# Building h in one kernel of a Griffin-style block: fourteen whole projection blocks, eight of them split, and first parts of fifteen mLSTM blocks

## The chip, the cores and the metric

The kernel runs on one core of a Trainium2 chip. The metric is the device time of one execution in microseconds (us); several runs are compared by their median. All data is fp32.

## The reference, cut to what matters

```python
mod = c_act @ ada_w + ada_b
shift_m, scale_m, gate_m, shift_f, scale_f, gate_f = jnp.split(mod[:, None, :], 6, axis=-1)
h = rms_norm(x, norm_mix_w) * (1 + scale_m) + shift_m
proj = h @ w_in
(a_q, a_k, a_v, a_o, a_i, a_f, b_qkv, b_z, b_beta, b_a, merge) = jnp.split(proj, IN_SPLITS, axis=-1)
...
h_a = bidirectional(mlstm_chunkwise, (q_a, k_a, v_a), (log_i[0], log_f[0]), (log_i[1], log_f[1]))
...
o_b = bidirectional(gated_delta_chunkwise, (q_b, k_b, v_b), (beta[0], log_decay[0]), (beta[1], log_decay[1]))
...
x = x + gate_m * ((g_a * y_a + g_b * y_b) @ w_out)
hf = rms_norm(x, norm_ffn_w) * (1 + scale_f) + shift_f
gt, up = jnp.split(hf @ w_gate_up, 2, axis=-1)
x = x + gate_f * ((jax.nn.silu(gt) * up) @ w_down)
```

There are 256 tokens, 2048 channels, 4 mLSTM heads (keys and queries of 256 channels) and 16 heads of the delta rule (GDN). The change lies in how the columns of `proj` are computed: one block row of 128 columns for the gates, 48 for the delta rule's k, q, v, and 16 for the mLSTM's keys and queries (two of each for a head).

## The kernel before, in words

**Building h.** h has 16 blocks `b` of 128 channels by 256 tokens. To modulate a block, DVE needs a scale and a shift for each of its channels: each is the sum of a row of 2048 weights times silu(c). These rows (`ra`, two tiles of 1 MB for each b, five buffers) stream from DRAM through SP's queue (function `loads`), DVE multiplies and sums them (`summed`, L548; `scale` is the first of the two calls). ACT then writes the block, `x[:, b]` (L587), and its value rounded to fp32r, `hh` (L588); DVE writes the remainder `hl` (L593), one step later than `hh`, and multiplies the next block by the norm's factor (`spread`, L553).

**The first projections.** While h is built, TensorE needs work: 16 block rows of `w_in` (N0; the gates, twelve for the first four GDN heads, three for the mLSTM's head 0) come with each b as a tile `raw` of 128 x 16 x 128 (1 MB, three buffers). For each, one fp32 matmul accumulates `raw[:, o]` times `x[:, b]` in one of 16 halves of the eight PSUM banks, `first[o]` (L595). In the last step only four block rows are done so; the twelve others are "split": ACT rounds the weights to `wh` (L603), DVE subtracts to get `wl` (L604), and three fp32r passes, wh·hh, wh·hl and wl·hh, take the place of one fp32 matmul (L606 to L608).

**Order.** `order()` keeps an instruction in the program's order among those of its engine that are also marked. Nearly all ACT and DVE instructions of this loop are marked. What isn't marked, the scheduler may place earlier. Each engine works through its queue in that order.

**After it.** `gates` computes decay and gates from `first[0]`, evicts `first[1..12]` to the convolution's pads (`evict`, L411), and copies the three mLSTM blocks to `ev0` and to DRAM, `kq_d[0]`. The remaining projections are jobs in a list, `fills`, of which the program takes a step (`fill(n)`) wherever the delta rule leaves TensorE free: `tjob` for wide ones (512 columns) and `fjob` for one block row. `fjob` (L172) loads 16 blocks (1 MB), splits eight at a time (ACT L181, DVE L183) and runs 48 passes (L186 to L188), with one `yield` for each eight blocks; `done` evicts the result. `a_qk(h, j)` is such a job for the mLSTM's keys and queries; before, 13 of them run (`rest`), with `keep_f` evicting to `evf` (two buffers) and ACT's queue storing to `kq_d`. `pump` in each step adds up further rows of the modulation. `mlstm(h)` loads `kq_d[h]` later through POOL's queue (L988), which also carries the delta rule's small transfers (`inst_d` L722 and others).

Of the kernel before, what the change touches and what calls it, by code (L numbers as in the profile page):

```python
# [9 lines left out]
F32 = mybir.dt.float32  # L10
# [5 lines left out]
P = 128  # L16
# [10 lines left out]
N0 = 4 + 3 * GRP  # L27
# [25 lines left out]
def hybrid_block(ctx: ExitStack, tc: tile.TileContext, xr, nfr, crow, pk_d, cst_d, ada2, ada4, win0, winb, wint, wba, wbb, wo, wgu, wd, out, dbg=None):  # L53
# [18 lines left out]
    def order(ins, yes=True):  # L72

        return tc.keep_in_program_order(ins) if yes else ins
# [97 lines left out]
    def fjob(name, src, done):  # L172

        ps = acc_ps.tile([P, 512], F32, tag="acc", name=f"acc_{name}")
        o = ps[:, :T]
        raw = raw_tile([P, KB, P], f"raw_{name}")
        nc.sync.dma_start(raw, src)
        for k0 in range(0, KB, 8):
            wh = st.tile([P, 8, P], F32R, tag="wh", bufs=3, name=f"wh_{name}_{k0}")
            wl = st.tile([P, 8, P], F32R, tag="wl", bufs=3, name=f"wl_{name}_{k0}")  # L180
            S.activation(wh, raw[:, k0 : k0 + 8], AF.Copy)  # L181
            settle()
            order(V.tensor_tensor(wl, raw[:, k0 : k0 + 8], wh.bitcast(F32), ALU.subtract), beside[0])  # L183
            for k in range(8):
                kk = k0 + k
                PE.matmul(o, wh[:, k], woven(hh[:, kk]), start=kk == 0, stop=False)  # L186
                PE.matmul(o, wh[:, k], woven(hl[:, kk]), start=False, stop=False)  # L187
                PE.matmul(o, wl[:, k], woven(hh[:, kk]), start=False, stop=kk == KB - 1)  # L188
            pump()
            if k0:  # L190
                done(o.rearrange("p (c h) -> p h c", h=2))
            yield True
# [179 lines left out]
    def keep_f(dst, name):  # L372
        def done(ps):
            ev = evp.tile([P, T], F32, tag="evf", bufs=2, name=f"ev_{name}")
            S.activation(ev.rearrange("p (h c) -> p h c", h=2), ps, AF.Copy)
            S.dma_start(dst, ev)
        return done
# [11 lines left out]
    def a_qk(h, j):  # L389
        return fjob(f"a{h}_{j}", winb[36 + 4 * h + j], keep_f(kq_d[h][j], f"a{h}_{j}"))  # L390
# [14 lines left out]
    for i in range(4):  # L405
        rest += [m_job(1, i), a_vo(1, i)] + [a_qk(i, j) for j in range(4) if i or j == 3] + [m_job(0, i)]

    def evict(o):

        if o <= 3 * GRP:  # L410
            S.activation(pads[(o - 1) % NP_][:, 2 : T + 2], first[o], AF.Copy)  # L411

    def gates(w0, zz, first):
# [75 lines left out]
        ev0 = w0.tile([P, D + 2], F32, tag="ra", bufs=5, name="ev0")  # L489
        for j in range(3):  # L490
            S.activation(ev0[:, j * T : (j + 1) * T], first[13 + j], AF.Copy)
        S.dma_start(kq_d[0][0:3].rearrange("j p t -> p j t"), ev0[:, : 3 * T].rearrange("p (j t) -> p j t", j=3))
# [14 lines left out]
    with ExitStack() as s0:  # L507
        w0 = pool(s0, "w0")

# [19 lines left out]
        def loads(b):  # L529
            ra = [w0.tile([P, D + 2], F32, tag="ra", bufs=5, name=f"ra{b}_{i}") for i in range(2)]  # L530
            raw = st.tile([P, N0, P], F32, tag="raw", bufs=3, name=f"raw0_{b}")
# [3 lines left out]
            n = 4 if b == KB - 1 else N0  # L535
            for o in range(0, N0, n):
                order(nc.sync.dma_start(raw[:, o : o + n], win0[b, :, o : o + n]))
            return ra, raw
# [16 lines left out]
        ra, raw = loads(0)  # L555
# [17 lines left out]
        banks += [gps(f"first{i}") for i in range(4, 8)]  # L573
# [4 lines left out]

        for b in range(KB):
            if b:  # L580
                ra, raw = loads(b)
                m2 = scale(b, ra)
# [6 lines left out]
            if b < KB - 1:  # L589
                spread(b + 1)  # L590
            for bb in ((b - 1,) if b < KB - 1 else (b - 1, b)):
                if bb >= 0:
                    order(V.tensor_tensor(hl[:, bb], x[:, bb], hh[:, bb].bitcast(F32), ALU.subtract))  # L593
            for o in range(N0 if b < KB - 1 else 4):
                PE.matmul(  # L595
                    first[o], raw[:, o], x[:, b], start=b == 0 and o % 2 == 0, stop=b == KB - 1 and o % 2 == 1
                )

        wh = [st.tile([P, 8, P], F32R, tag="wh", bufs=3, name=f"wh_first{i}") for i in range(2)]
        wl = [st.tile([P, 8, P], F32R, tag="wl", bufs=3, name=f"wl_first{i}") for i in range(2)]  # L600
        for o0 in range(4, N0, 4):
            w = [a[o0 // 8][:, o0 % 8 : o0 % 8 + 4] for a in (wh, wl)]
            order(S.activation(w[0], raw[:, o0 : o0 + 4], AF.Copy))  # L603
            order(V.tensor_tensor(w[1], raw[:, o0 : o0 + 4], w[0].bitcast(F32), ALU.subtract))  # L604
            for o in range(o0, o0 + 4):
                PE.matmul(first[o], w[0][:, o - o0], hh[:, KB - 1], start=False, stop=False)  # L606
                PE.matmul(first[o], w[0][:, o - o0], hl[:, KB - 1], start=False, stop=False)
                PE.matmul(first[o], w[1][:, o - o0], hh[:, KB - 1], start=False, stop=o % 2 == 1)  # L608


        nc.sync.dma_start(pk, pk_d)
        zz = w0.tile([P, T], F32, name="zz")
        opened = gates(w0, zz, first)
# [998 lines left out]
def _arrays(x, c, ada_w, ada_b, norm_mix_w, w_in, mlstm_b_i, mlstm_b_f, mlstm_norm_w, gdn_conv_w,  # L1612
# [32 lines left out]
    for h in range(NH_A):  # L1645
# [24 lines left out]
        "win0": np.ascontiguousarray(win[[*range(13), 49, 50, 51]].transpose(2, 1, 0, 3)),  # L1670
# [25 lines left out]
```

## Time and profile before

| | |
|---|---|
| median of 3 runs | 1948.41 us (1947.84 to 1948.59) |
| profiled execution | 1949.3 us, its span 1947.4 us |
| PE busy | 1920.7 us (99%) |
| DVE, ACT, POOL busy | 1406.5 (72%), 1032.7 (53%), 124.1 us (6%) |
| moved by DMA | 485.68 MB, mean 249 GB/s |
| the loop over b | first matmul at 19.28 us, last one of the stage at 135.63 us |

The span runs from the first to the last instruction; the run's time lies 1.9 us above it. PE is TensorE's matmuls, PEld its weight loads, DVE VectorE, ACT ScalarE, POOL GpSimd, SP the engine whose queue issues most loads. A busy share is an average over stages: the building of h is limited by other things than the rest. In a line in order of time stand the start and the length in us, the engine, the line of the code (L595), the operation, the written and read tiles, and in brackets how long the engine had been idle and what released it.

### The profile page before, as it was taken

To read this page: it belongs to the slowest core of one execution; us is meant where nothing else is said; L and a number is where in the kernel's file an instruction comes from. 1 tells how busy PE (TensorE), PEld (TensorE's weight loads), DVE (VectorE), ACT (ScalarE), POOL (GpSimd) and SP (SyncE) were. 2 spreads that over 40 slices of the span, in tenths; PEclk is the share of its full clock that TensorE was granted. 3 is DMA by queue.
4 is the path that set the end of the run, shared out by engine and by line. 5 is a ranking of instruction groups with operands and counts; after the bars stand their busy time and mean duration, and the time that the engine had idled before them with its cause. 6 is when DMAs were issued, how large, how long until landed. Compare 5 with 4: busy or idle time off the path is not lost.

```text
span 1947.4 us, 27209 instructions
## 1 busy us (share of the span) xinstructions
PE 1920.7 (99%) x10436; PEld 1704.7 (88%) x10436; DVE 1406.5 (72%) x2084; ACT 1032.7 (53%) x1564; POOL 124.1 (6%) x223
## 2 busy tenths in 40 slices
PE   8999999999999999999999999999999999999997
PEld 7888889998999899889788888888888888888886
DVE  6788886898788789877577988765665655555554
ACT  3147656765776587565544444644444444444443
POOL 0001220111011101120100000200000000000000
PEclk9999999999999999999999999999999999999999
DMA  9997676666666767686777998577677665565553
GB/s 398 421 358 236 188 257 247 207 230 226 233 213 206 244 216 237 208 296 243 254 290 267 357 348 322 201 248 253 242 251 258 240 218 198 205 206 210 196 208 136
DMA packets 80773, 485.68 MB, mean 249 GB/s; under 512 B 11433, under 2 KB 17137, under 8 KB 26625
## 3 DMA queue, kind: packets, MB, share of 16 engines
q1 hardware_dynamic: 64368, 451.02, 64.2%
q0 software_dynamic: 8672, 17.88, 4.4%
q10 hardware_dynamic: 7602, 15.03, 2.0%
q8 instruction: 82, 1.34, 0.3%
q14 instruction: 49, 0.40, 0.1%
HBM read 467.07 MB, written 16.82 MB: 248 GB/s over the span
## 4 chain that ended last, share of the span: by engine, by line
PE 88%; DVE 4%; DMA 4%; ACT 2%; issue 1%; POOL 0%; SPq 0%; DVEq 0%; POOLq 0%
PE acc_up L249 4%; PE acc_up L248 4%; PE acc_up L247 4%; PE acc_gt L248 4%; PE acc_d L248 4%; PE acc_gt L249 4%; PE acc_d L247 4%; PE acc_d L249 4%; PE acc_gt L247 4%; DMA ra<-ada 3%; PE acc_b L186 3%; PE acc_b L188 3%; PE acc_b L187 3%; PE acc_o L247 2%; PE acc_o L249 2%; PE acc_o L248 2%
## 5 line engine op out<-in xcount | busy, mean ns | idle before, releaser
L215 DVE TENSOR_TENSOR wl_d<-raw_d,wh_d 128x1024 fp32r<-128x1024 f32 x88 | 107.7, 1225 | 105.9 <-ACT wh_d L213 105.9
L215 DVE TENSOR_TENSOR wl_up<-raw_up,wh_up 128x1024 fp32r<-128x1024 f32 x88 | 107.7, 1225 | 100.7 <-ACT wh_up L213 100.7
L215 DVE TENSOR_TENSOR wl_gt<-raw_gt,wh_gt 128x1024 fp32r<-128x1024 f32 x88 | 107.7, 1224 | 76.9 <-ACT wh_gt L213 76.9
L186 PE MATMUL acc_b<-hh,wh_b 128*128 128x256 f32 x576 | 162.7, 283 | 0.0
L213 ACT ACTIVATE wh_d<-raw_d 128x1024 fp32r<-128x1024 f32 x88 | 92.9, 1056 | 126.8 <-PE acc_d L248 118.0
L188 PE MATMUL acc_b<-hh,wl_b 128*128 128x256 f32 x576 | 159.4, 277 | 0.1
L187 PE MATMUL acc_b<-hl,wh_b 128*128 128x256 f32 x576 | 159.1, 276 | 0.0
L213 ACT ACTIVATE wh_gt<-raw_gt 128x1024 fp32r<-128x1024 f32 x88 | 92.9, 1056 | 121.7 <-PE acc_gt L248 75.7
L213 ACT ACTIVATE wh_up<-raw_up 128x1024 fp32r<-128x1024 f32 x88 | 92.8, 1056 | 108.0 <-PE acc_up L248 77.0
L125 DVE SCALAR_TENSOR_TENSOR ada<-ada,crow 128x2048 f32<-128x2048 f32 x64 | 146.2, 2284 | 0.0
L247 PE MATMUL acc_up<-wh_up,hfh 128*128 128x512 f32 x352 | 133.4, 379 | 0.0
L248 PE MATMUL acc_up<-wh_up,hfl 128*128 128x512 f32 x352 | 133.4, 379 | 0.0
L249 PE MATMUL acc_up<-wl_up,hfh 128*128 128x512 f32 x352 | 133.4, 379 | 0.0
L247 PE MATMUL acc_gt<-wh_gt,hfh 128*128 128x512 f32 x344 | 131.6, 383 | 0.0
L248 PE MATMUL acc_gt<-wh_gt,hfl 128*128 128x512 f32 x344 | 130.5, 379 | 0.3 <-DVE hfl L1473 0.3
L248 PE MATMUL acc_d<-wh_d,ffl 128*128 128x512 f32 x344 | 130.5, 379 | 0.0
L249 PE MATMUL acc_gt<-wl_gt,hfh 128*128 128x512 f32 x344 | 130.4, 379 | 0.0
L247 PE MATMUL acc_d<-wh_d,ffh 128*128 128x512 f32 x344 | 130.4, 379 | 0.0
L249 PE MATMUL acc_d<-wl_d,ffh 128*128 128x512 f32 x344 | 130.4, 379 | 0.0
L595 PE MATMUL first<-x,raw 128*128 128x256 f32 x488 | 109.5, 385 | 5.4 <-ACT x L587 5.4
L595 PEld LDWEIGHTS first<-x,raw 128*128 128x128 f32 x488 | 93.0, 192 | 22.0 <-ACT x L587 9.4
L187 PEld LDWEIGHTS acc_b<-hl,wh_b 128*128 128x128 f32 x576 | 111.4, 193 | 0.1
(403 smaller groups left out, 5296.1 us busy)
## 6 DMA issues: line engine op xcount, KB each, us to landing
ada<-ada SPq DMA_DIRECT2D x64, 1024.0 KB, 5.0
raw_gt<-wgu SPq DMA_DIRECT2D x44, 1024.0 KB, 4.9
raw_up<-wgu SPq DMA_DIRECT2D x44, 1024.0 KB, 4.9
raw_d<-wd SPq DMA_DIRECT2D x44, 1024.0 KB, 4.8
raw_b<-winb SPq DMA_DIRECT2D x36, 1024.0 KB, 5.2
ra<-ada SPq DMA_DIRECT2D x30, 1025.0 KB, 14.9
raw_z<-wint SPq DMA_DIRECT2D x16, 1024.0 KB, 4.9
raw_v<-wint SPq DMA_DIRECT2D x16, 1024.0 KB, 5.4
```

Of the source, the lines that this page charges most:

```text
L125: order(V.scalar_tensor_tensor(raw, raw, 1.0, row_c[:, :D], ALU.mult, ALU.mult, accum_out=mod[:, c : c + 1]))
L186: PE.matmul(o, wh[:, k], woven(hh[:, kk]), start=kk == 0, stop=False)
L187: PE.matmul(o, wh[:, k], woven(hl[:, kk]), start=False, stop=False)
L188: PE.matmul(o, wl[:, k], woven(hh[:, kk]), start=False, stop=kk == KB - 1)
L213: order(S.activation(wh, raws[u][:, k0 : k0 + 2], AF.Copy), early)
L215: order(V.tensor_tensor(wl, raws[u][:, k0 : k0 + 2], wh.bitcast(F32), ALU.subtract), early or beside[0])
L247: order(PE.matmul(ps[t], xh[:, kk, c], woven(wh[:, k]), start=kk == 0, stop=False), early and steps > 1)
L248: PE.matmul(ps[t], xl[:, kk, c], woven(wh[:, k]), start=False, stop=False)
L249: PE.matmul(ps[t], xh[:, kk, c], woven(wl[:, k]), start=False, stop=kk == last)
L595: PE.matmul(first[o], raw[:, o], x[:, b], start=b == 0 and o % 2 == 0, stop=b == KB - 1 and o % 2 == 1)
```

## The change

The loop now carries 14 block rows: the gates, the twelve of the first four GDN heads, and one mLSTM key block. Six of them (NPL) stay fp32 matmuls; the other eight are split in every step, so ACT makes `wh` and DVE `wl` for 128 x 1024 weights in each. Since the passes of step b read `hl[:, b]`, `hl` is now made in the same step. Results of split blocks lie with even and odd tokens apart in PSUM, and the evictions reorder them.

The 14 rows take seven banks. In the eighth (`apart`), steps b = 3 to 13 compute first parts of the 15 other mLSTM blocks: two blocks each for b = 3 to 6, of their first four channel blocks, and one each for b = 7 to 13, of its first eight. Their weights (`ex`, 512 KB a step) are loaded after `raw` into two buffers that later stages own (`sz`, `ev`), and split too. `put` evicts a step's parts on ACT in the next step to `some`, which is stored to `kq_d` by four transfers after the loop; the gates' small tiles (pool `w1`) take over its memory. The 15 jobs `a_qk` (13 before) then begin at channel block 4 or 8 (`k0` in `fjob`), and their result is added to the one in DRAM by a transfer of POOL's queue (`accum_op`). The eleven steps with partial blocks add 88 blocks of 128 x 128 to the loop, while the jobs have 152 where they had 208.

```diff
FB = FF // P
...
 GRP = 4
-N0 = 4 + 3 * GRP
+N0 = 14
+NPL = 6
...
 PK_ADAB = 0
...
         if more:
...
-    def fjob(name, src, done):
+    def fjob(name, src, done, k0=0):
...
         raw = raw_tile([P, KB, P], f"raw_{name}")
-        nc.sync.dma_start(raw, src)
-        for k0 in range(0, KB, 8):
-            wh = st.tile([P, 8, P], F32R, tag="wh", bufs=3, name=f"wh_{name}_{k0}")
-            wl = st.tile([P, 8, P], F32R, tag="wl", bufs=3, name=f"wl_{name}_{k0}")
-            S.activation(wh, raw[:, k0 : k0 + 8], AF.Copy)
+        nc.sync.dma_start(raw[:, k0:], src[:, k0:])
+        first_ = k0
+        while k0 < KB:
+            k1 = min(k0 + 8 - k0 % 8, KB)
+            wh = st.tile([P, 8, P], F32R, tag="wh", bufs=3, name=f"wh_{name}_{k0}")[:, : k1 - k0]
+            wl = st.tile([P, 8, P], F32R, tag="wl", bufs=3, name=f"wl_{name}_{k0}")[:, : k1 - k0]
+            S.activation(wh, raw[:, k0:k1], AF.Copy)
             settle()
-            order(V.tensor_tensor(wl, raw[:, k0 : k0 + 8], wh.bitcast(F32), ALU.subtract), beside[0])
-            for k in range(8):
-                kk = k0 + k
-                PE.matmul(o, wh[:, k], woven(hh[:, kk]), start=kk == 0, stop=False)
+            order(V.tensor_tensor(wl, raw[:, k0:k1], wh.bitcast(F32), ALU.subtract), beside[0])
+            for kk in range(k0, k1):
+                k = kk - k0
+                PE.matmul(o, wh[:, k], woven(hh[:, kk]), start=kk == first_, stop=False)
                 PE.matmul(o, wh[:, k], woven(hl[:, kk]), start=False, stop=False)
...
             pump()
-            if k0:
+            k0 = k1
+            if k0 == KB:
                 done(o.rearrange("p (c h) -> p h c", h=2))
...
             S.dma_start(dst, ev)
...
-    def keep_f(dst, name):
+    def keep_f(dst, name, more=True):
         def done(ps):
...
             S.activation(ev.rearrange("p (h c) -> p h c", h=2), ps, AF.Copy)
-            S.dma_start(dst, ev)
+            if more:
+                G.dma_start(dst, ev, accum_op=ALU.add)
+            else:
+                S.dma_start(dst, ev)
         return done
...
     def z_job(g, early=0):
...
         return fjob(f"b{h}_{j}", winb[3 * (h - GRP) + j], lambda ps: gdn_conv(h, j, ps))
...
     def a_qk(h, j):
-        return fjob(f"a{h}_{j}", winb[36 + 4 * h + j], keep_f(kq_d[h][j], f"a{h}_{j}"))
+        e = 4 * h + j - 1
+        return fjob(f"a{h}_{j}", winb[37 + e], keep_f(kq_d[h][j], f"a{h}_{j}"), 4 if e < 8 else 8)
...
         return tjob(
...
     for i in range(4):
-        rest += [m_job(1, i), a_vo(1, i)] + [a_qk(i, j) for j in range(4) if i or j == 3] + [m_job(0, i)]
+        rest += [m_job(1, i), a_vo(1, i)] + [a_qk(i, j) for j in range(4) if i or j] + [m_job(0, i)]
...
         if o <= 3 * GRP:
-            S.activation(pads[(o - 1) % NP_][:, 2 : T + 2], first[o], AF.Copy)
+            pd = pads[(o - 1) % NP_][:, 2 : T + 2]
+            if o < NPL:
+                S.activation(pd, first[o], AF.Copy)
+            else:
+                S.activation(pd.rearrange("p (h c) -> p h c", h=2), first[o].rearrange("p (c h) -> p h c", h=2), AF.Copy)
...
         evict(1)
...
         V.tensor_copy(tr[96:104], ex[R, :, 1])
-        ev0 = w0.tile([P, D + 2], F32, tag="ra", bufs=5, name="ev0")
-        for j in range(3):
-            S.activation(ev0[:, j * T : (j + 1) * T], first[13 + j], AF.Copy)
-        S.dma_start(kq_d[0][0:3].rearrange("j p t -> p j t"), ev0[:, : 3 * T].rearrange("p (j t) -> p j t", j=3))
+        keep_f(kq_d[0][0], "a0_0", False)(first[13].rearrange("p (c h) -> p h c", h=2))
         gdn_conv(1, 1, None)
...
         ptr = gps("ptr")
...
         w0 = pool(s0, "w0")
+        se = ExitStack()
+        we = pool(se, "we")
+        some = we.tile([P, 15, T], F32, name="some")
+        beside_h = {3 + i: [(2 * i, 4), (2 * i + 1, 4)] for i in range(4)}
+        beside_h.update({7 + i: [(8 + i, 8)] for i in range(7)})
...
         ss = w0.tile([P, 2], F32, name="ssx")
...
             ra = [w0.tile([P, D + 2], F32, tag="ra", bufs=5, name=f"ra{b}_{i}") for i in range(2)]
-            raw = st.tile([P, N0, P], F32, tag="raw", bufs=3, name=f"raw0_{b}")
+            raw = st.tile([P, KB, P], F32, tag="raw", bufs=3, name=f"raw0_{b}")
             for i in range(2):
...
                     order(nc.sync.dma_start(ra[i][:, c], ada2[b, :, i, c]))
-            n = 4 if b == KB - 1 else N0
-            for o in range(0, N0, n):
-                order(nc.sync.dma_start(raw[:, o : o + n], win0[b, :, o : o + n]))
-            return ra, raw
+            for c in (slice(0, NPL), slice(NPL, 10), slice(10, N0)) if b == KB - 1 else (slice(0, N0),):
+                order(nc.sync.dma_start(raw[:, c], win0[b, :, c]))
+            ex = None
+            if b in beside_h:
+                ex = evp.tile([P, 2, 512], F32, tag=("sz", "ev")[b % 2], bufs=1, name=f"ex{b}").rearrange("p a (k c) -> p (a k) c", c=P)
+                for i, (e, n) in enumerate(beside_h[b]):
+                    order(nc.sync.dma_start(ex[:, i * n : (i + 1) * n], winb[37 + e][:, :n]))
+            return ra, raw, ex
...
             m2 = w0.tile([P, 2, 2], F32, tag="m2", bufs=3, name=f"m2_{b}")
...
         def spread(b):
...
-        ra, raw = loads(0)
+        ra, raw, ex = loads(0)
         m2 = scale(0, ra)
...
         dg = w0.tile([P, T], F32, name="dgx")
...
         order(S.activation(rows, prow[:, :T], AF.Copy))
...
         banks = [acc_ps.tile([P, 512], F32, tag="acc", name=f"first{i}") for i in range(4)]
-        banks += [gps(f"first{i}") for i in range(4, 8)]
+        banks += [gps(f"first{i}") for i in range(4, 7)]
+        apart = gps("apart")
         first = [banks[o // 2][:, (o % 2) * T : (o % 2 + 1) * T] for o in range(N0)]
...
+        def parts_of(name, src):
+            w = [st.tile([P, 8, P], F32R, tag=t, bufs=3, name=f"{t}_{name}") for t in ("wh", "wl")]
+            n = src.shape[1]
+            order(S.activation(w[0][:, :n], src, AF.Copy))
+            return [a[:, :n] for a in w]
+
+        def rest_of(w, src):
+            order(V.tensor_tensor(w[1], src, w[0].bitcast(F32), ALU.subtract))
+
+        def low(b):
+            order(V.tensor_tensor(hl[:, b], x[:, b], hh[:, b].bitcast(F32), ALU.subtract))
+
+        def passes(o, w, n, b, start, stop):
+            PE.matmul(o, w[0][:, n], woven(hh[:, b]), start=start, stop=False)
+            PE.matmul(o, w[0][:, n], woven(hl[:, b]), start=False, stop=False)
+            PE.matmul(o, w[1][:, n], woven(hh[:, b]), start=False, stop=stop)
+
+        def put(b):
+            for i, (e, n) in enumerate(beside_h.get(b, ())):
+                S.activation(
+                    some[:, e].rearrange("p (h c) -> p h c", h=2),
+                    apart[:, i * T : (i + 1) * T].rearrange("p (c h) -> p h c", h=2), AF.Copy,
+                )
+
         for b in range(KB):
+            end = b == KB - 1
             if b:
-                ra, raw = loads(b)
+                ra, raw, ex = loads(b)
                 m2 = scale(b, ra)
...
                 summed(b, ra[1], 1.0, m2[:, 1])
...
                 spread(0)
...
             order(S.activation(hh[:, b], x[:, b], AF.Copy))
-            if b < KB - 1:
+            put(b - 1)
+            if not end:
                 spread(b + 1)
-            for bb in ((b - 1,) if b < KB - 1 else (b - 1, b)):
-                if bb >= 0:
-                    order(V.tensor_tensor(hl[:, bb], x[:, bb], hh[:, bb].bitcast(F32), ALU.subtract))
-            for o in range(N0 if b < KB - 1 else 4):
-                PE.matmul(
-                    first[o], raw[:, o], x[:, b], start=b == 0 and o % 2 == 0, stop=b == KB - 1 and o % 2 == 1
-                )
-
-        wh = [st.tile([P, 8, P], F32R, tag="wh", bufs=3, name=f"wh_first{i}") for i in range(2)]
-        wl = [st.tile([P, 8, P], F32R, tag="wl", bufs=3, name=f"wl_first{i}") for i in range(2)]
-        for o0 in range(4, N0, 4):
-            w = [a[o0 // 8][:, o0 % 8 : o0 % 8 + 4] for a in (wh, wl)]
-            order(S.activation(w[0], raw[:, o0 : o0 + 4], AF.Copy))
-            order(V.tensor_tensor(w[1], raw[:, o0 : o0 + 4], w[0].bitcast(F32), ALU.subtract))
-            for o in range(o0, o0 + 4):
-                PE.matmul(first[o], w[0][:, o - o0], hh[:, KB - 1], start=False, stop=False)
-                PE.matmul(first[o], w[0][:, o - o0], hl[:, KB - 1], start=False, stop=False)
-                PE.matmul(first[o], w[1][:, o - o0], hh[:, KB - 1], start=False, stop=o % 2 == 1)
-
+            else:
+                low(b)
+            for o in range(NPL):
+                PE.matmul(first[o], raw[:, o], x[:, b], start=b == 0 and o % 2 == 0, stop=end and o % 2 == 1)
+            for c in (slice(NPL, 10), slice(10, N0)) if end else (slice(NPL, N0),):
+                w = parts_of(f"first{b}_{c.start}", raw[:, c])
+                rest_of(w, raw[:, c])
+                if not end:
+                    low(b)
+                for o in range(c.start, c.stop):
+                    passes(first[o], w, o - c.start, b, b == 0 and o % 2 == 0, end and o % 2 == 1)
+            if ex is not None:
+                w = parts_of(f"ex{b}", ex)
+                rest_of(w, ex)
+                for i, (e, n) in enumerate(beside_h[b]):
+                    for k in range(n):
+                        passes(apart[:, i * T : (i + 1) * T], w, i * n + k, k, not i and not k, k == n - 1 and i == len(beside_h[b]) - 1)
+
+        for h in range(NH_A):
+            e = range(max(4 * h - 1, 0), 4 * h + 3)
+            S.dma_start(kq_d[h][4 - len(e) :].rearrange("j p t -> p j t"), some[:, e.start : e.stop])
+        se.close()
+        w1 = pool(s0, "w1")
         nc.sync.dma_start(pk, pk_d)
-        zz = w0.tile([P, T], F32, name="zz")
-        opened = gates(w0, zz, first)
+        zz = w1.tile([P, T], F32, name="zz")
+        opened = gates(w1, zz, first)
         next(opened)
...
         zj = z_job(0, 2)
...
         "cst": cst,
...
         "ada4": np.ascontiguousarray(adaT[2:]),
-        "win0": np.ascontiguousarray(win[[*range(13), 49, 50, 51]].transpose(2, 1, 0, 3)),
+        "win0": np.ascontiguousarray(win[[*range(13), 49]].transpose(2, 1, 0, 3)),
         "winb": np.ascontiguousarray(win[13:]),
...
```

## The prediction

> **What bounds the kernel now.** I read the page first, then the stretches, then the instructions in order of time. The page gives busy time by engine, and the chain that ended last by engine:
>
> ```profile
> PE 1920.7 (99%) x10436; PEld 1704.7 (88%) x10436; DVE 1406.5 (72%) x2084; ACT 1032.7 (53%) x1564; POOL 124.1 (6%) x223
> ...
> PE 88%; DVE 4%; DMA 4%; ACT 2%; issue 1%; POOL 0%; SPq 0%; DVEq 0%; POOLq 0%
> ```
>
> TensorE carries nearly all of the span, so a matmul that disappears from the later stages is worth its own time. The stage that the change rebuilds is different. The table of stretches (PE, PEld, DVE, ACT, POOL busy, then PEclk, DMA share, GB/s) has for the building of h:
>
> ```profile
> 26.30:122.70 96.40, 93.57 (x424) 79.49 (x422) 69.38 (x78) 12.81 (x26) 0.00 (x0) 1.00 1.01 420
> ```
>
> The DMA engines are full at 420 GB/s, PE is close behind them, DVE is busy for 69.4 of 96.4 us, and ACT hardly works. One step of the loop over b, in order of time:
>
> ```profile
> 64.83 2.35 DVE L548 SCALAR_TENSOR_TENSOR ra<-ra,pkn,crow 128x2050 f32<-128x2050 f32 x1 [2.20 <-DMA ra<-ada]
> ...
> 69.55 0.42 DVE L553 TENSOR_TENSOR x<-x,rows 128x256 f32<-128x256 f32 x1
> 69.67 0.60 ACT L587 ACTIVATE x<-x,m 128x256 f32<-128x256 f32 x1 [6.62 <-DVE ra L548]
> ...
> 69.89 0.42 DVE L593 TENSOR_TENSOR hl<-x,hh 128x256 fp32r<-128x256 f32 x1
> ...
> 70.30 0.42 ACT L588 ACTIVATE hh<-x 128x256 fp32r<-128x256 f32 x1
> 70.32 7.17 PE L595 MATMUL first<-x,raw 128*128 128x256 f32 x32 [0.50 <-ACT x L587]
> 72.30 2.35 DVE L548 SCALAR_TENSOR_TENSOR ra<-ra,pkn,crow 128x2050 f32<-128x2050 f32 x1 [2.00 <-DMA ra<-ada]
> ...
> 77.34 0.42 DVE L593 TENSOR_TENSOR hl<-x,hh 128x256 fp32r<-128x256 f32 x1
> ```
>
> The step takes 7.47 us (64.83 to 72.30), and DVE ends each with about 2 us of idling for `ra`. In that time it could have formed `hl` of the block whose `hh` ended at 70.72; it does so only at 77.34, behind the next two sums. So the hand-written order of `order()` is really kept on DVE, even against an idle engine. That is what my forecast turns on.
>
> **The change, part by part.**
>
> *Matmul work.* Two block rows (32 blocks of 128x128) leave the loop, 88 partial blocks enter it (8 x 4 and 7 x 8), and 56 leave the later jobs: thirteen jobs of 16 make 208, eight of 12 and seven of 8 make 152. What a block costs later is read from one such job, and what it costs in the loop from the twelve split blocks at its end:
>
> ```profile
> 900.43 0.28 PE L186 MATMUL acc_a<-hh,wh_a 128*128 128x256 f32 x1
> ...
> 902.11 0.28 PE L186 MATMUL acc_a<-hh,wh_a 128*128 128x256 f32 x1
> ```
> ```profile
> 131.25 0.47 PE L606 MATMUL first<-hh,wh_first 128*128 128x256 f32 x1
> ...
> 135.75 0.38 PE L247 MATMUL acc_z<-wh_z,hh 128*128 128x512 f32 x1
> ```
>
> The first pair lies five blocks apart: 1.68 / 5 = 0.336 us per block. Where PE is the bound, 56 x 0.336 = 18.8 us go. In the loop a whole fp32 block costs 7.17 / 16 = 0.448 us, a split one 0.336 to (135.75 - 131.25) / 12 = 0.375 us. A full step then has 6 x 0.448 + 16 x 0.336 to 0.375 = 8.1 to 8.7 us of PE.
>
> *Loads.* The loop loads 56 blocks of 64 KB more, 3.67 MB; at 420 GB/s that is 8.7 us if DMA stays the bound. A full step moves 2.10 + 0.92 + 0.52 = 3.54 MB, 8.4 us.
>
> *DVE and ACT.* Each step now has an ACT copy and a DVE subtraction of 128x1024 for the eight split blocks, and eleven steps (b = 3 to 13) another pair for the partial blocks. `hl` moves from the step after to the step itself, between the two subtractions. All these are ordered on their engines. ACT runs x, hh, the evictions `put` of the step before, then the two copies; DVE runs the two sums, `spread`, the first subtraction, `hl`, the second, and only then the next sums. So DVE, which has the sums of the next block landed and waiting, must first wait for ACT to come through x, hh, `put` and a copy, and ACT can't start before the sums of this step. This is a new loop through two engines, without a slot in which either works ahead. Its links come from these rows:
>
> ```profile
> L213 ACT ACTIVATE wh_z<-raw_z 128x1024 fp32r<-128x1024 f32 x8 | 8.2, 1049 | 0.9 <-PE acc_z L248 0.7
> L215 DVE TENSOR_TENSOR wl_z<-raw_z,wh_z 128x1024 fp32r<-128x1024 f32 x8 | 9.6, 1218 | 0.0
> L375 ACT ACTIVATE ev_a<-acc_a 128x256 f32<-128x256 f32 x13 | 4.8, 367 | 0.5 <-PE acc_a L188 0.5
> ```
> ```profile
> 128.72 0.60 ACT L587 ACTIVATE x<-x,m 128x256 f32<-128x256 f32 x1 [5.62 <-DVE m L550]
> 129.35 0.42 ACT L588 ACTIVATE hh<-x 128x256 fp32r<-128x256 f32 x1
> 129.68 1.65 ACT L603 ACTIVATE wh_first<-raw 128x512 fp32r<-128x512 f32 x3
> ...
> 130.32 1.90 DVE L604 TENSOR_TENSOR wl_first<-raw,wh_first 128x512 fp32r<-128x512 f32 x3
> ...
> 136.21 2.35 DVE L215 TENSOR_TENSOR wl_z<-raw_z,wh_z 128x1024 fp32r<-128x1024 f32 x2
> ```
>
> Let S be the start of `spread`. x starts at S + 0.12, hh at S + 0.75 (69.55, 69.67, 70.30). The copy follows 0.33 behind hh (129.35 to 129.68) and takes 1.05: done at S + 2.13. The subtraction starts right behind it; I take 0.03 (the first of three copies that last 1.65 together was done near 130.29, an estimate, and its subtraction began at 130.32). Two of 128x1024 take 2.35 and one 1.22 us, so the next instruction starts 1.13 behind: `hl` at S + 3.29, and what follows it 0.34 later (69.55 to 69.89), S + 3.63. From the first sum to `spread` it is 4.72 (64.83 to 69.55). A step without partial blocks is thus 8.35 us, one with them 8.35 + 1.13 = 9.48, and every `put` ahead of the copy adds 0.36 (0.37 is its near relation, the `ev_a` row). Against the step of 7.47, and against the 8.4 that DMA would set, the loop through ACT is the later one.
>
> Now the stage from its start. In the trace:
>
> ```profile
> 18.77 2.35 DVE L548 SCALAR_TENSOR_TENSOR ra<-ra,pkn,crow 128x2050 f32<-128x2050 f32 x1 [0.75 <-DMA ra<-ada]
> 19.26 0.42 ACT L588 ACTIVATE hh<-x 128x256 fp32r<-128x256 f32 x1
> ...
> 123.47 1.28 DVE L548 SCALAR_TENSOR_TENSOR ra<-ra,pkn,crow 128x1024 f32<-128x1024 f32 x1 [0.79 <-DMA ra<-ada]
> ```
>
> With hh of block 0 at 19.26, the copy ends at 20.64, the subtraction runs from 20.67, `hl` from 21.80, and the sums of b = 1 start at 22.14 instead of 18.77; S(1) = 26.86. Then two steps of 8.35 (b = 1, 2), one of 9.48 (b = 3, no `put` yet), four with two `put` of 10.20 (b = 4 to 7), six with one of 9.84 (b = 8 to 13): S(14) = 26.86 + 16.70 + 9.48 + 40.80 + 59.04 = 152.88. Step 14 has no partial blocks but the last `put`: the sums of b = 15 start 3.99 later, at 156.87, against 123.47. That is 33.4 us late. The tail gets slightly shorter: before, 7.03 us pass from x of block 15 (128.72) to the first matmul of the z job (135.75); now PE starts 0.65 after x (69.67 to 70.32) and has 6 x 0.448 + 8 x 0.375 = 5.69 us, in all 6.34. The stage costs 32.7 us more.
>
> PE is not the bound in this: its passes need `hl`, so in a step with two `put` they start at S + 4.4, and 47 of 0.125 end at S + 10.3 at the latest, 1 us before the next step's `put` asks for the bank (S + 10.20 + 1.08).
>
> *The later stages.* The thirteen evictions become fifteen and stay beside PE. The stores move from ACT's queue to POOL's, as additions in DRAM. Rows for that, POOL's groups and the list of waits:
>
> ```profile
> L722 POOL DMA_DIRECT2D inst_d<-mi x64 | 35.1, 555 | 385.6 <-DVE mi L716 385.4
> L988 POOL DMA_DIRECT2D mkq<-kq_d x4 | 3.0, 760 | 0.4 <-issue 0.4
> ...
> POOL inst_d L722 <- DVE mi L716: 385.4, 16, 57.0
> ```
>
> Fifteen issues of 0.56 to 0.76 us are 8 to 11 us on an engine that is 94% idle: nothing on the path. What could hurt is the queue: an addition behind an `inst_d` that waits for DVE (up to 57 us) keeps one of the two `evf` buffers, the third eviction then holds ACT, and behind it the copies on which PE lives. I take 0, with up to 8 us as the other end, about three jobs' worth of 16 x 0.336.
>
> The Trainium skill's page "SBUF — State Buffer", sections "SBUF: two separate sides" and the one behind it on bandwidth pools, speaks against moving stores to this queue: POOL can't write descriptors while DVE runs a two-port operation, and it gives about 3100 ns for a transfer that takes 620 ns alone. Fifteen of these would be 37 us more of POOL time, an estimate from that page, which by itself would still lie beside PE. The rows of 555 and 760 ns come from stretches with a busy DVE and do not show such a block, so it moves only the chance of the queue's rival a little.
>
> The small tiles of the gates now reuse the memory of `some`, so zz waits for its four stores. Their data is complete at the last `put` (about 154.3 by the sum above), while zz waits for PE's first blocks of b = 15, near 163.7; if they are issued only behind the last copies on ACT, zz is some 5 us late, and ACT and PE with it. I take 0 and keep 5.
>
> *Sum.* 1949.3 us (profiled execution; its span is 1947.4) + 32.7 - 18.8 = 1963.2. The median of the runs is 0.9 below the profiled one, so 1962.3.
>
> **Rivals.**
>
> *Loads set the pace: faster.* If copies and subtractions find room beside the sums, DMA stays the bound and the stage costs 8.7 us more instead of 32.7; with 18.8 saved the kernel takes 1948.4 - 10.1 = 1938.3. The break-even is an average step of 7.47 + 18.8 / 15 = 8.7 us. For it: DVE's own work in a full step is 4.72 + 2 x 0.34 + 2 x 1.13 = 7.7 us, ACT's under 4. Against it: nothing in the order lets the next sums pass the subtractions, and the 2 us of idling with `hl` ready show that DVE doesn't reorder. The skill's page "Perfetto Trace Analysis", section "Identifying the Most-Contended Engine", has one take the bottleneck from occupancy; by it the full DMA would go on bounding this stage, which is this rival.
>
> *Half hidden.* If the wait on ACT is half as long (for instance because `put` and the copies start earlier than I place them), the stage costs about 20.7 us and the total is near 1950.
>
> *More than the stage: slower still.* Either the stores of `some` or the additions behind POOL's waits cost 5 to 8 us, or the shortened jobs no longer cover the delta-rule work between them, so that only about 12 of the 18.8 us are realised. Each gives 1967 to 1971.
>
> That the change doesn't do what it says could only be the last one: fewer matmuls without less time.
>
> **How the numbers follow.** Forecast 0.62, loads set the pace 0.14, half hidden 0.10, slower still 0.14. Predicted is the likeliest, 1962.3; its own range is 1957 to 1967. The range of 1947 to 1972 takes in the half-hidden case and the slower ones, and leaves out the faster rival and a few beyond 1972. About 0.2%, 3.9 us, is what can be told from no change. Faster: the first rival and a little of the second, 0.15. Within: half of the half-hidden case, 0.05. Slower: 0.80.
>
> **What the profile would show.** Right: steps of about 10 us for b = 4 to 13, each with DVE idle some 2 us before `wl_first` with ACT named as releaser, where before it idled for `ra`; DMA share clearly under 1 (8.4 / 10 = 0.84) in the stretch; the last x of the stage near 162; `acc_a` matmuls 208 to 152 per line. Wrong: DVE still idling for `ra` with the DMA share at 1, steps under 8.7 us; or PE waiting for long on `wh` or `ev_a` between 300 and 950; or zz waiting for a store.

## The result, and the profile after

| | before | after |
|---|---|---|
| median of 5 runs | 1948.41 us (1947.84 to 1949.65) | 1979.21 us (1976.53 to 1981.76) |
| profiled execution, span | 1949.3, 1947.4 us | 1979.21, 1977.4 us |
| first matmul of the z job | 135.7 us | 163.4 us |

The changed kernel takes 1.016 times as long (1.0149 to 1.0172): 30.8 us more, where 13.9 were forecast, and beyond the stated range of 1947 to 1972. On its page, the lines that answer to those shown of before:

```profile
PE 1916.1 (97%) x10584; PEld 1704.9 (86%) x10584; DVE 1426.0 (72%) x2106; ACT 1056.0 (53%) x1602; POOL 138.2 (7%) x238
...
PE 79%; DVE 6%; issue 5%; DMA 5%; ACT 4%; POOL 1%; ACTq 0%; DVEq 0%; SPq 0%; POOLq 0%
```

TensorE is busy for 4.6 us less, in a span 30.0 us longer, and its share of the chain falls from 88% to 79%: other engines hold it up. One step of the loop over b, in order of time:

```profile
60.94 0.42 DVE L571 TENSOR_TENSOR x<-x,rows 128x256 f32<-128x256 f32 x1
61.17 0.66 ACT L617 ACTIVATE some<-apart 128x256 f32<-128x256 f32 x2 [6.11 <-PE apart L613]
...
62.02 0.60 ACT L631 ACTIVATE x<-x,m 128x256 f32<-128x256 f32 x1 [0.19 <-ACT some L617]
62.52 1.04 ACT L601 ACTIVATE wh_first<-raw 128x1024 fp32r<-128x1024 f32 x1
63.47 0.40 ACT L632 ACTIVATE hh<-x 128x256 fp32r<-128x256 f32 x1
...
63.60 1.23 DVE L605 TENSOR_TENSOR wl_first<-raw,wh_first 128x1024 fp32r<-128x1024 f32 x1 [2.23 <-ACT wh_first L601]
64.74 0.42 DVE L608 TENSOR_TENSOR hl<-x,hh 128x256 fp32r<-128x256 f32 x1
65.08 1.22 DVE L605 TENSOR_TENSOR wl_ex<-ex,wh_ex 128x1024 fp32r<-128x1024 f32 x1
66.21 2.35 DVE L566 SCALAR_TENSOR_TENSOR ra<-ra,pkn,crow 128x2050 f32<-128x2050 f32 x1
...
70.70 0.42 DVE L571 TENSOR_TENSOR x<-x,rows 128x256 f32<-128x256 f32 x1
```

The step takes 9.76 us. DVE idles 2.23 us for ACT's copy, as forecast. But ACT does not start with x: the evictions `put` (L617), which `order()` does not mark, stand ahead of x, and ACT waits 6.11 us for PE's last partial pass before them. The list of waits has both:

```profile
ACT some L617 <- PE apart L613: 67.0, 11, 6.1
...
DVE wl_first L605 <- ACT wh_first L601: 27.9, 15, 2.6
```

Behind the loop, TensorE's own waits (total, times, longest) have new entries (1.8 of the 6.8 us lie at the start of the z job). First the rows of after, then what the list of before has on the same tiles; `px` is not in it:

```profile
PE acc_z L251 <- ACT wh_z L217: 6.8, 3, 2.5
PE px L951 <- DVE on L978: 3.6, 1, 3.6
...
PE acc_a L191 <- DVE wl_a L186: 2.6, 1, 2.6
```
```profile
PE acc_z L249 <- DVE wl_z L215: 2.5, 3, 1.0
...
PE acc_a L188 <- DVE wl_a L183: 0.4, 1, 0.4
```

To see what such a wait costs, I split the span: the start of the z job, and the stretch from the first matmul of `acc_a` to the first of `acc_yb`, in which all mLSTM jobs lie. "Idle" sums the time there in which no matmul runs; "clock" sums 1 minus the granted clock over stretches of 5 us.

| kernel | z starts | `acc_a` to `acc_yb` | idle | clock |
|---|---|---|---|---|
| before | 135.7 | 664.8 | 5.0 | 3.4 |
| after | 163.4 | 666.8 | 17.4 | 11.9 |
| E1 new loop, old jobs | 161.6 | 661.8 | 4.0 | 1.7 |
| E2 old loop, short jobs | 135.5 | 664.4 | 16.3 | 10.2 |
| E5 new loop reordered | 152.3 | 666.4 | 17.9 | 11.9 |
| E6 E2, short steps | 135.7 | 661.8 | 17.7 | 3.4 |
| E7 before, fewer steps | 135.5 | 672.6 | 8.0 | 8.5 |
| E9 E2, steps as before | 135.7 | 657.6 | 11.8 | 8.5 |
| E10 E5 and E9 | 150.5 | 654.8 | 11.6 | 5.1 |
| E12 after, `put` marked | 163.4 | 666.1 | 17.0 | 11.9 |

For after, 18.8 us less of matmuls, 12.4 more idle and 8.5 more by the clock make +2.1; the stretch is 2.0 us longer. So two things were to be explained: +27.7 at the start, and a saving that vanished.

### The profile page after: what moved, and what is told of

Same layout as the page of the kernel before. It is cut to its first block, busy times and chain, and to the rows that moved or that the text cites. A ratio compares the mean times of both kernels' runs of the same rounds, so it can differ in the third digit from the quotient of the medians.

```text
span 1977.4 us, 27628 instructions
## 1 busy us (share of the span) xinstructions
PE 1916.1 (97%) x10584; PEld 1704.9 (86%) x10584; DVE 1426.0 (72%) x2106; ACT 1056.0 (53%) x1602; POOL 138.2 (7%) x238
## 4 chain that ended last, share of the span: by engine, by line
PE 79%; DVE 6%; issue 5%; DMA 5%; ACT 4%; POOL 1%; ACTq 0%; DVEq 0%; SPq 0%; POOLq 0%
PE acc_up L251 4%; PE acc_up L253 4%; PE acc_up L252 4%; PE acc_gt L252 4%; PE acc_d L252 4%; PE acc_d L251 4%; PE acc_gt L253 4%; PE acc_d L253 4%; PE acc_gt L251 4%; PE acc_b L189 3%; PE acc_b L191 3%; PE acc_b L190 3%; PE acc_o L251 2%; PE acc_o L252 2%; PE acc_o L253 2%
## 5 line engine op out<-in xcount | busy, mean ns | idle before, releaser
L189 PEld LDWEIGHTS acc_b<-hh,wh_b 128*128 128x128 f32 x576 | 110.6, 192 | 0.1
L191 PEld LDWEIGHTS acc_b<-hh,wl_b 128*128 128x128 f32 x576 | 110.6, 192 | 0.0
```

Source lines behind the costliest of these rows:

```text
L189: PE.matmul(o, wh[:, k], woven(hh[:, kk]), start=kk == first_, stop=False)
```

## The experiments

Times are medians of 4 runs, for E2, E6, E9 and E11 of 10; ratios are to the kernel before on the same chip (its median there 1946.4 to 1948.5 us), with the 95% interval.

| | us | ratio to before |
|---|---|---|
| E1 | 1973.30 | 1.0129 (1.0112 to 1.0146) |
| E2 | 1947.59 | 0.9996 (0.9987 to 1.0006) |
| E3 | 1976.73 | 1.0147 (1.0130 to 1.0163) |
| E4 | 1976.85 | 1.0145 (1.0130 to 1.0160) |
| E5 | 1968.68 | 1.0106 (1.0089 to 1.0123) |
| E6 | 1951.57 | 1.0021 (1.0011 to 1.0030) |
| E7 | 1955.17 | 1.0038 (1.0023 to 1.0053) |
| E8 | 1969.61 | 1.0114 (1.0099 to 1.0130) |
| E9 | 1941.97 | 0.9973 (0.9964 to 0.9983) |
| E10 | 1959.57 | 1.0057 (1.0042 to 1.0072) |
| E11 | 1943.46 | 0.9979 (0.9970 to 0.9989) |
| E12 | 1979.70 | 1.0172 (1.0154 to 1.0189) |

**E1 and E2: each half alone.** E1 keeps the new loop and the old thirteen jobs; E2 keeps the old loop and shortens the jobs. Neither computes the whole block: in E2, and in E6, E9 and E11, which build on it, the first parts of the mLSTM's keys and queries are missing. Their times show the schedule and are no versions to use.

```diff
# E1, against after
-... keep_f(kq_d[h][j], f"a{h}_{j}"), 4 if e < 8 else 8)
+... keep_f(kq_d[h][j], f"a{h}_{j}", False))
-    ... for j in range(4) if i or j] ...
+    ... for j in range(4) if i or j == 3] ...
# E2, against before: fjob with k0, a_qk from k0 = 4 or 8
-    ... for j in range(4) if i or j == 3] ...
+    ... for j in range(4) if i or j] ...
```

> The new loop with the thirteen whole jobs of before and their plain stores (mLSTM head 0's second key block and first query block then hold only their first parts). Measures the loop's price alone. The traces say 27 to 28 us (the z job's first matmul moved from 135.7 to 163.4), so 1976; the prediction's own sum said 32.7, so 1981. If the new loop also disturbs the later stages (rival: a shifted schedule), more than 1983.

> The loop of before with the fifteen shortened jobs, plainly stored by ACT's queue (the first parts of the mLSTM keys and queries are missing). Three theories of where the 18.8 us of removed matmuls went. Cover: the jobs lose three of their 26 steps and some steps are half as long, so the delta rule's chains lie open; then little is saved here too, 1944 to 1950. Queue: POOL's additions hold the eviction buffers; there are none here, so 1930. Shifted schedule: the loss comes with the new loop; 1930 as well.

E1 is 24.8 us above before, E2 1.0 below: 56 blocks fewer bring nothing. E2's list of TensorE's waits has the new entries of after, without the new loop and without additions in DRAM:

```profile
PE acc_z L250 <- ACT wh_z L216: 5.0, 2, 2.5
PE px L906 <- DVE on L933: 3.6, 1, 3.6
...
PE acc_a L190 <- DVE wl_a L185: 2.4, 1, 2.4
```

The halves add up to 24, not 30.8. What the other 7 us are was not separated; among them are a wait for `raw_z` ahead of the z job (1.8 us in after), and 3.0 us by which E1's stretch is shorter than that of before, with less idling and less clock lost, of which after shows nothing.

**E3: plain stores.**

```diff
-            if more:
-                G.dma_start(dst, ev, accum_op=ALU.add)
-            else:
-                S.dma_start(dst, ev)
+            S.dma_start(dst, ev)
```

> The changed kernel with plain stores by ACT's queue instead of POOL's additions in DRAM (the first parts are overwritten, not added). Queue theory: 12 to 19 us faster than the changed kernel, 1960 to 1967. Cover theory: at most the 5 us that ACT waited for additions, 1974 to 1979.

1976.73 us, 2.5 under after, with intervals that overlap: POOL's queue is at most a small part of the loss, and E2 has the loss without it. In after, the transfers of `ev_a` read:

```profile
L381 POOL DMA_DIRECT2D kq_d<-ev_a x15: 850/900/967, 326.8 to 937.8; - x15
...
DMA to landing us min/median/max: 3.1/6.5/9.5
```

An addition costs POOL 0.90 us to issue and lands in 6.5 us (median of the 15 and one plain store), where the plain stores of before landed in 4.3 and those of E3 in 4.6. ACT waited for a buffer behind one (5.1 us in two waits, 3.9 in E3), so that wait does not need the additions.

**E4, E5, E12: the order of ACT's queue in the loop.** E12 marks `put` alone, so that it stands behind hh, as the prediction had it. E4 puts both copies ahead of x and leaves `put` unmarked. E5 gives ACT the order: first copy, x, hh, second copy, `put`.

```diff
# E12, against after (E5 has it too)
-                S.activation(
+                order(S.activation(
                     some[:, e]...
# E5 (E4 makes both copies here)
+            ws = [] if end else [parts_of(f"first{b}", raw[:, NPL:N0])]
             order(S.activation(x[:, b], ...))
             order(S.activation(hh[:, b], x[:, b], AF.Copy))
+            if ex is not None:
+                ws.append(parts_of(f"ex{b}", ex))
             put(b - 1)
```

> The changed kernel with ACT's two copies of a step issued before x instead of behind it and behind put, so that DVE finds them made. If the loop through ACT is what makes a step 9 to 9.8 us, steps fall to the pace of DMA, 8.4, and the kernel is 10 to 16 us faster than the changed one: 1963 to 1969. If PE and the evictions of its bank set the step, it gains under 5: 1974 or more.

> The changed kernel with another order on ACT in a step: wh_first, x, hh, wh_ex, and only then put, all marked. In the changed kernel put, unmarked, stands ahead of x and waits for PE's last pass into the bank apart (67 us of ACT's waits), so x waits for PE and PE then for x. Theory PE-put-x ring: freed of it a step falls from 9.2 to 9.75 us to the pace of DMA, 8.4 to 8.6; the z job starts 10 to 14 us sooner and the kernel takes 1964 to 1970. Rival, the loop through DVE and the copies alone sets the step (as predicted): no more than 4 us, 1974 to 1979.

> The changed kernel with put marked and nothing else: ACT's order is then the one that the prediction assumed, x, hh, put, wh_first, wh_ex. The ring over PE is gone, the ring of DVE and the copies is whole. By the prediction's step, with 4.49 us for two sums without a wait for DMA: 9.25 + 0.36 for each put, so 9.6 to 10 us a step against 9.2 to 9.75 measured in the changed kernel; the z job starts 1 to 6 us later than its 163.4 and the kernel takes 1978 to 1986. If PE's ring alone was what held the step, it gains 8 us or more, as e5 did: under 1972.

E12, in order of time and in the list of waits of the stage:

```profile
91.28 0.60 ACT L631 ACTIVATE x<-x,m 128x256 f32<-128x256 f32 x1 [6.31 <-DVE ra L566]
...
92.50 1.05 ACT L601 ACTIVATE wh_first<-raw 128x1024 fp32r<-128x1024 f32 x1
...
93.58 1.23 DVE L605 TENSOR_TENSOR wl_first<-raw,wh_first 128x1024 fp32r<-128x1024 f32 x1 [2.00 <-ACT wh_first L601]
```
```profile
ACT x L631 <- DVE ra L566: 87.7, 14, 6.3
```

ACT now waits for the sums and DVE for ACT: the forecast ring, with `spread` every 9.52 us with one `put` and 9.79 with two (10.20 in the first of these). The time does not fall, 1979.70. So the ring through PE in after (9.07 to 10.12 us a step) only stands in front of one of nearly the same length: from b = 5 to b = 14 the mean step is 9.49 us in after and 9.61 in E12. E4 breaks the second ring but only half of the first: `put` and x follow behind PE's last partial pass as before (ACT's wait for it falls from 67.0 to 29.8 us), and 1976.85 us can't be told from after. It also has waits of its own, so it does not test the second ring alone: the second copy now waits for PE to be done with a weight buffer, and PE then waits for that copy.

```profile
PE apart L611 <- ACT wh_ex L601: 14.4, 7, 4.0
ACT wh_ex L601 <- PE first L612: 12.3, 4, 5.2
```

E5 frees both rings. Its wait list and its stretches (PE, PEld, DVE, ACT, POOL busy, PEclk, DMA share, GB/s), and those of after:

```profile
ACT wh_first L601 <- DMA raw<-win: 71.1, 13, 7.3
```
```profile
48.00:128.00 80.00, 73.60 (x529) 68.93 (x528) 68.11 (x73) 29.97 (x49) 0.00 (x0) 0.98 1.01 408
```
```profile
40.00:140.00 100.00, 85.05 (x617) 79.67 (x617) 79.42 (x86) 35.05 (x58) 0.00 (x0) 1.00 0.94 371
```

In E5 the loads set the pace, with the DMA engines full, and the z job starts 11.1 us earlier than in after; the time falls by about as much, to 1968.68. Its loop still costs 16.6 us more than that of before. Of this, the 3.67 MB of added loads and the 1.97 MB of `some` (15 tiles of 128 KB), most of it stored while the loop runs, make 13.8 us at 408 GB/s (an estimate); the rest was not separated.

**E6, E7: only the number of steps.** `fill(n)` takes steps of the list, not matmuls. Before, the thirteen mLSTM jobs gave 26 steps; the fifteen shorter ones give 23, and four more of them come for head 0 and seven fewer for heads 2 and 3. E7 is the kernel before with the same matmuls, but three late jobs yield once, which makes 23. E6 is E2 with steps of four blocks in the seven shorter jobs, which makes 30.

```diff
# E7, against before
-            yield True
+            if k0 or not once:
+                yield True
# E6, against E2; step = 8 if e < 8 else 4
-            k1 = min(k0 + 8 - k0 % 8, KB)
+            k1 = min(k0 + step - k0 % step, KB)
```

> The kernel of e2 (loop of before, shortened jobs, plain stores), but the seven shortest jobs hand over after four blocks instead of eight: thirty steps instead of 23, the same matmuls. If the lost time is the number of steps (the list runs out before the delta rule ends, and job ends fall on other chain steps), some 8 to 15 us come back: 1933 to 1940. If it is the amount of matmul work between the chain's steps, nothing comes back: 1945 to 1950.

> The kernel before with all its matmuls, but the last three mLSTM jobs hand over once in 16 blocks instead of twice: 23 steps instead of 26. If the number of steps is what counts, the list runs out early and the last pair of heads lies open: 4 to 10 us slower, 1952 to 1958. If the amount of work counts, no change: 1947 to 1950.

E7 is slower by 7.6 us with not one matmul changed, and shows the wait of after to the tenth. Its list of waits, then two stretches at the end of the list of before and of E7:

```profile
PE px L903 <- DVE on L930: 3.6, 1, 3.6
```
```profile
945.00:960.00 15.00, 15.00 (x50) 8.06 (x50) 5.20 (x11) 7.53 (x17) 2.79 (x5) 0.89 0.81 295
```
```profile
945.00:960.00 15.00, 12.06 (x38) 8.45 (x39) 3.09 (x15) 4.32 (x12) 2.56 (x4) 0.66 0.51 179
```

Before, the last matmul of the list is followed by that of `px` without a gap (944.2 us). In E7 the list is empty by then, PE waits for the delta rule's own chain, and the clock granted in the stretch is 0.66 where it was 0.89. The wait of 3.6 us and the clock lost in these 15 us, 3.5 more than before, make 7.1 of the 7.8 us by which the stretch from `acc_a` to `acc_yb` grew. (The other 1.7 us of clock in the table lie from 370 to 385 us, far ahead of the edited jobs.) E6 has no wait at `px`, and its stretch is 3.0 us shorter than that of before (661.8), but the z waits remain (5.0 us), and behind the stretch, from `acc_yb` to `acc_ya`, it takes 112.1 us where before takes 104.9. There it has 4.2 us of idling and 3.4 of clock more; nearly all of the idling is one wait:

```profile
PE acc_yb L250 <- ACT wh_yb L216: 3.9, 1, 3.9
```

1951.57 is no gain, and slightly above what was expected for a number of steps without effect. So a larger number of steps does not help by itself.

**E9, E11: as many steps as before, at the same places.** E9 is E2 with two jobs of head 0 moved to the third group, one of them in one step, and steps of four blocks for head 3; so it changes the order and the size of steps with their number. E11 cuts its jobs of twelve blocks into 8 and 4 instead of 4 and 8.

```diff
# E9, against E2; step = 4 if h == 3 else 8, once = (e == 1)
-            yield True
+            if k0 == KB or not once:
+                yield True
-    ... for j in range(4) if i or j] + ...
+    ... for j in range(4) if i or j == 3] + [a_qk(0, j) for j in (1, 2) if i == 2] + ...
# E11, against E9
-            k1 = min(k0 + step - k0 % step, KB)
+            k1 = min(k0 + step, KB)
```

> The kernel of e2 (loop of before, shortened jobs, plain stores) with as many steps at each place of the list as before: two of head 0's jobs go from the first group to the third (three steps), head 3's hand over after four blocks. If the saving was lost because the steps no longer lie where the delta rule's chain needs them, the long gaps at the z jobs and at the last pair go and half or more of the 18.8 us comes back: 1932 to 1940. If shorter steps by themselves leave the chains open, under 4 us: 1944 to 1950.

> e9 with the jobs of twelve blocks cut into eight and four instead of four and eight, so that the step ahead of a chain's wait is the long one. The gap of 2.4 us at the first head-1 job behind the second inversion should go: 2 to 4 us faster than e9. If that gap is set by DVE and not by the step's length, no change.

E9 is 5.8 us under before, and E11 4.3. For E9 that lies between the two expectations: less than a third of the 18.8 us comes back, so number and place of the steps are a part of what was lost, and its stretch still has 6.8 us more idling and 5.1 more clock lost than before. The waits of `acc_z` for `wh_z` and of `px` are gone; one wait at `acc_a` grew:

```profile
PE acc_a L190 <- DVE wl_a L185: 4.8, 1, 4.8
```
```profile
489.13 0.71 DVE L791 STREAM_TRANSPOSE cg<-cg 128x512 f32<-128x512 f32 x1 [6.17 <-DMA cg<-inv_d]
...
490.78 1.22 DVE L185 TENSOR_TENSOR wl_a<-raw_a,wh_a 128x1024 fp32r<-128x1024 f32 x1
```

DVE stands in its queue in front of a transpose that waits for the inversion's transfer, and the subtraction for the next step lies behind it. Before, with jobs of 16 blocks, PE has 0.4 us of waiting there; with the jobs of 12 blocks that stand there in E9 it has 4.8. E11's larger first step was expected to take this gap away and leaves it (5.2 us): how it could be covered stays open.

**E8, E10: the cures together.** E8 is E5 with the steps of E6; E10 is E5 with the list of E9, additions included (diffs as above).

> e5's order in the loop and e6's steps in the jobs, on the changed kernel with its additions. Both theories right: 1948 to 1958. Only the order: 1964 to 1970. Only the steps: 1964 to 1972. Neither: 1975 to 1980.

> The same list of steps with e5's order in the loop and POOL's additions: the whole change, mended in both places. Steps theory: e5's 1968.7 less what e9 gains over e2, 1953 to 1961. Otherwise 1964 to 1970. Faster than before only if e9 gains all of it and the loop another 3 us.

E8 gains nothing over E5. E10 has the stretch at 654.8, 10.0 under before, and the z job 14.8 later: 1959.57 us, the fastest version here with the whole change, 19.6 under after and still 1.0057 times before. (The two alone would make 4.8; the rest of the 11.8 us was not separated.) No version that computes everything beats the kernel before.

## Why the prediction was wrong

The direction was right, the size was not. The forecast was +32.7 for the loop and -18.8 for the jobs.

**The term that failed: "Where PE is the bound, 56 x 0.336 = 18.8 us go."** The blocks did go; by tile:

```profile
L189 PE MATMUL acc_a<-hh,wh_a x152: 272/275/421, 321.4 to 933.0; 128*128 128x256 f32 x152
```

But the stretch grew by 2.0 us. The jobs are also the cover of the delta rule, in steps, and the prediction counted matmuls without asking where the steps lie and what the delta rule waits for beneath them. Its "slower still" rival named the mechanism, "the shortened jobs no longer cover the delta-rule work", but granted 12 of the 18.8; nothing remained. One of its signs of being wrong came: between 300 and 950 us PE waits 5.0 us for `wh_z`. E2 shows the loss without the loop, E7 shows without any shortening that fewer steps alone cost 7.6 us, and E9 wins a part back by the number and the places of the steps; for the rest, the idling and the clock are measured, but which of the shorter steps opens which gap was followed at single places only. One such place in after, in order of time:

```profile
454.17 0.84 ACT L955 ACTIVATE obt<-px,pk 128x256 f32<-128x256 f32 x2 [1.52 <-PE px L951]
...
455.53 1.06 ACT L217 ACTIVATE wh_z<-raw_z 128x1024 fp32r<-128x1024 f32 x1 [0.52 <-ACT obt L955]
...
456.64 0.48 PE L251 MATMUL acc_z<-wh_z,hh 128*128 128x512 f32 x1 [2.51 <-ACT wh_z L217]
```

The copy for the z job stands on ACT behind the delta rule's `obt`, and PE has nothing else. (Before, that copy was made at 431.05 us, ahead of `obt` at 433.00, and the z job followed `px` without a gap.) The forecast also had no price for the clock:

```profile
450.00:455.00 5.00, 4.13 (x22) 3.38 (x20) 2.85 (x15) 3.41 (x7) 0.00 (x0) 1.00 0.45 185
455.00:460.00 5.00, 2.26 (x6) 1.65 (x7) 4.67 (x10) 4.41 (x10) 2.18 (x4) 0.79 0.24 67
460.00:465.00 5.00, 5.00 (x14) 3.87 (x14) 2.85 (x3) 1.24 (x2) 1.29 (x3) 0.53 0.71 232
```

Idle gaps of 2.51 and 1.11 us are followed by 5 us in which PE is busy throughout and is granted 0.53 of its clock: 14 matmuls, where the stretch from 465 has 25.

**The loop: right within 5 us, partly for other reasons.** z started 27.7 us later, not 32.7. The last x came at 155.4, not 162.1, and then 8.0 us passed to z, not 6.3, with the wait for `raw_z` in them. The ring of DVE and ACT's copy exists: E12 has it alone. It was over-sized: the sums to `spread` take 4.49 us (66.21 to 70.70), where the 4.72 of before held a 0.2 us wait for loads, and a `put` delays the copy by 0.26 (92.24 to 92.50), not 0.36. That makes steps of 9.5 and 9.8 instead of 9.84 and 10.20. That the loop's figure came out so near is in part luck: the ring that held the steps of after is not the one that was summed, but one through PE that happens to be nearly as long. What the prediction read wrongly is `put`'s place: it took an instruction without a mark to stay where the program has it, though the description of `order()` says that such instructions may go earlier. The DMA share, forecast at 0.84, was 0.94 from 40 to 140.

**The rivals.** "Loads set the pace" is not what after does, but it becomes true in E5; there the loop costs 16.6 us, not 8.7; the stores of `some`, 1.97 MB and most of them inside it, are some 4.8 us of the difference by the rate of 408 GB/s (an estimate). The Trainium skill's page "Perfetto Trace Analysis", section "Identifying the Most-Contended Engine", takes the engine with the highest occupancy as the bottleneck, with the use of HBM in place of occupancy for DMA. In after DMA is the fullest by its busy share, 0.94 (371 GB/s), and yet E5's order takes 11.1 us off, so the waits decide here. The price on POOL's queue finds little room in E3, 2.5 us. Most stores of `some` run in the loop, where the prediction expected them behind it, and zz was not late for them: it began at 158.2 us, when DVE had finished its last subtraction. But each of them held SP's queue once, as the waits of that queue in after show:

```profile
SPq L550 <- DMA kq_d<-some: 15.8, 1, 15.8
SPq L555 <- DMA kq_d<-some: 15.5, 1, 15.5
SPq L548 <- DMA kq_d<-some: 11.1, 1, 11.1
SPq L660 <- DMA kq_d<-some: 8.8, 1, 8.8
```

In the loop this cost nothing that shows (DVE waited 0.7 us for loads in all). Behind it the first `raw_z` was issued only at 155.93 us, 7.5 ahead of the z job (before at 124.73, 11.0 ahead), and z waited 1.8 us for it; in E1, with the same hold, 0.2. So the stores had a price at another tile than zz, small beside the 5 us that were kept for it.

## What to carry to other kernels

Work that fills the gaps of another chain is worth its own time only while the chain stays covered: before cutting it, list the gaps, the filler's steps in each, and what the next step needs from engines that are queued behind the chain. When a list is shortened, look to the number and the places of its steps (keeping both brought 5.8 of 18.8 us here), and read the stretch, not the busy time. When work is moved into a loop, look for each pair of engines that wait for each other within one step, and mark every instruction whose place matters: two rings of nearly the same length hide each other, and taking away one showed nothing here.

## What the runs showed of the hardware

In windows of 1 us the granted clock reads 0.50 throughout the falls looked at: from 458 to 464 us in after, from 378 to 380 and from 948 to 950 in before. The entries of the table's last column are all near whole multiples of 1.7 us (2 of them in before, 7 in after), which is what 3.4 us at 0.50 lose.

The clock fell after gaps shorter than I had reckoned with. The Trainium skill's page "TensorE: Matmul & The Clock Gate", section "What's actually happening", has the array go to half rate after an idle window of about 3.4 us. The half rate and the length fit. The gaps in front don't: at 456 us in after they were 2.51 and 1.11 us, apart from each other, and the fall at 948 in before comes without any, right behind the small matmuls of `px` and `pden` (PE is busy for 15.00 of the 15 us in the line shown for 945 to 960). Here the measurement decides; what does release such a fall, no run here shows.

So there is no fixed price for an idle microsecond. In after the idle time and the lost clock stand at 12.4 and 8.5 us above before; in E6 the idle time of the same stretch is 12.7 us above before, and the lost clock is no larger.

Additions in DRAM from POOL's queue took 0.85 to 0.97 us to issue, and landed about 2 us later than plain stores from ACT's queue (6.5 against 4.3 and 4.6 us). How much of that is the addition and how much the queue was not separated.
